# A hybrid trunk on one core: layer 3's block copies all on ScalarE, its chains' zero fills all on GpSimd

## The chip, the core and the metric

One core of a Trainium2 chip. The metric is the device time of one execution, in microseconds; the median of three runs stands for the kernel.

## The reference, cut to what matters

A trunk of four layers over 256 latent and 256 context tokens, width 1024, float32. Each layer has a token mixer (latent attention, differential attention, gated linear attention, gated DeltaNet) and a squared-ReLU MLP. The change lies in the mixer of layer 3, the gated delta rule, in chunks of 64 tokens, 16 value heads, both directions:

```
lmat  = where(strict, (k*beta) @ k^T * gamma, 0)         # 64x64 per chunk, head and direction
t_inv = triangular_solve(lmat, eye, lower, unit_diagonal) # its inverse
u, w  = t_inv @ (v*beta), t_inv @ (k*beta*exp(gc))
step:   v_new = u_c - w_c @ s;  o = q_c @ s + a_c @ v_new;  s = s*d_c + k_c^T @ v_new
```

The inverses are needed for 256 matrices of 64x64 (4 chunks, 16 heads, 2 directions, 2 streams of tokens), and the recurrence over chunks then uses them.

## The kernel before, in words

`run` goes through layers 0 to 2, then opens layer 3 with `gdn_products` and `gdn_scans`, and ends with the MLP of layer 3.

`gdn_products` makes the projections of layer 3 and solves for the inverses in two groups of eight heads. The projections come as jobs (k, q, v and z of one head each). A v job is 24 matmuls on TensorE (L296 to L298, weights split into a high and a low part by ScalarE's cast L279 and VectorE's subtraction L280), a convolution (L1387 on ScalarE, then four L1390 on VectorE), SiLU on ScalarE, four transposes on TensorE (L1585) and scalings on ScalarE (L1588), and a store by GpSimd's queue (L1589). A z job is eight matmuls (L1544) and a SiLU. `GDN_PLAN` says how many jobs the code puts beside each step of a solve.

`gdn_solve(grp)` has three parts.

- Setup. For each pass p (0 and 1: which half runs forward) and each pair of chunks t it masks the gates of eight heads on VectorE (L1408), sums them on TensorE (L1411), takes the exponential on ScalarE (L1413) and multiplies into the matrix `lm[p]` on VectorE (L1414, L1415). `lm[0]` lies in buffer `xd`, `lm[1]` in `xb`. Each 64x64 matrix is then taken apart into two 32x32 diagonal blocks (`xc`, in buffer `xa`, L1434) and one off-diagonal block (`lo`, L1436). One copy moves 32 partitions x 1024 elements. In L1434 ScalarE and VectorE copy in turn (q even: ScalarE, q odd: VectorE), four copies per pass; in L1436 one each per pass. Two transposes of VectorE (L1439) follow; they write `x`, which takes the buffer `xb` again and so has to wait until `lm[1]` has been read.
- Loop. 31 steps of forward substitution on VectorE (L1444 and L1446), with jobs beside them.
- Join. Four transposes on VectorE (L1450, L1451), then for both passes k small 32x32 matmuls on TensorE (L1460), evacuated by ScalarE (L1463), the diagonal blocks copied into the result `uc` (L1469: four copies per k, b = 0 on ScalarE, b = 1 on VectorE), zeros into its upper block by GpSimd (L1470), a second set of small matmuls (L1476), evacuated by ScalarE with a sign (L1478), and a store of `uc` to memory by GpSimd's queue (L1481).

`gdn_scans` opens its buffers, fills the zero halves of the block-diagonal tiles once (L1837: four `uc` tiles on VectorE, three `at` tiles on GpSimd, two fills of 64 partitions x 512 elements each), and runs the chains (`gdn_chain`), which load the stored `uc` into the other halves (L1618, SyncE's queue) and multiply with them on TensorE (L1653), with ScalarE (L1657) and VectorE (L1650, L1672) between.

The order of the instructions of an engine is not the order of the code. A planner orders each engine's queue when the program is built, by the place in the code, by when the operands are ready in its own model of costs, and by free buffers: in the trace the first copies of pass 0 (L1434) run from 2070.2 us on, before pass 1's products, which stand ahead of them in the code. Buffers are counted: three rows for the setup's products (`side`), two PSUM banks for the sums and the small matmuls (`st`).

Of the kernel before, what the change touches and what calls it, by code (L numbers as in the profile page):

```python
# [157 lines left out]
class Trunk:  # L158
# [1234 lines left out]
    def gdn_solve(self, grp):  # L1393


        nc = self.nc
        lm = [self.x4.tile([128, 32, 64], F32, name=("xd", "xb")[p]) for p in range(2)]
# [25 lines left out]
        xc, v = both("xa"), both("xc")  # L1423
        quad = lambda a, b: slice(64 * a + 32 * b, 64 * a + 32 * b + 32)

        lo = self.lpool.tile([128, 32, 32], F32, name="lo")
# [3 lines left out]
        for p in passes:  # L1430
            nc.gpsimd.memset(v[:, p].rearrange("p i j -> p (i j)")[:, ::33], 1.0)
            for q in range(4):
                b = 32 * (q % 2)
                (nc.vector.tensor_copy if q % 2 else nc.scalar.copy)(xc[32 * q:32 * q + 32, p], lm[p][32 * q:32 * q + 32, :, b:b + 32])  # L1434
            for a in range(2):
                (nc.vector.tensor_copy if a else nc.scalar.copy)(lo[quad(a, p)], lm[p][quad(a, p), :, 32 * (1 - p):32 * (1 - p) + 32])  # L1436
        x = both("xb")
        for p in passes:
            nc.vector.transpose(out=low(x[:, p], p), in_=sw(xc[:, p]))  # L1439
# [8 lines left out]
        un, ut = both("xd"), both("xa")  # L1448
# [16 lines left out]
        for k in passes:  # L1465
            uc = self.x4.tile([128, 32, 64], F32, name=("xc", "xa")[k])
            for a in range(2):
                for b in range(2):
                    (nc.vector.tensor_copy if b else nc.scalar.copy)(uc[quad(a, b), :, 32 * b:32 * b + 32], un[quad(a, b), k])  # L1469
                nc.gpsimd.memset(uc[quad(a, 1 - k), :, 32 * k:32 * k + 32], 0.0)  # L1470
            for u0 in (0, 16):
                zp = self.st.tile([128, T2], F32, name="st")
                for u in range(16):
                    for a in range(2):
                        src, dst = quad(a, 1 - k), quad(a, k)
                        nc.tensor.matmul(zp[dst, 32 * u:32 * u + 32], lhsT=y[src, k, u0 + u], rhs=un[src, k, u0 + u], start=True, stop=True)  # L1476
                for a in range(2):
                    nc.scalar.mul(uc[quad(a, k), u0:u0 + 16, 32 * (1 - k):32 * (1 - k) + 32],  # L1478
                                  zp[quad(a, k)].rearrange("p (u c) -> p u c", c=32), -1.0)
                yield  # L1480
            nc.gpsimd.dma_start(self.spill[f"uc{grp}{k}"], uc)  # L1481
# [340 lines left out]
    def gdn_scans(self):  # L1822
        nc = self.nc
        with ExitStack() as ctx:
            pool = self.opener(ctx)
            self.open_psum(pool, **GDN_BANKS)
            banks = self.accs
            self.acc = lambda: banks.tile([128, T2], F32, name="acc")
            self.vp, self.ktk = pool("gdnv", GDN_ROWS2[4]), pool("gdnkt", GDN_ROWS2[5])

            diag = pool("gdnd2", 1)
            self.diag = {}
            for name, n in (("uc", GDN_ROWS2[1]), ("at", GDN_ROWS2[2])):
                ts = [diag.tile([128, 2, 4, 2, 64], F32, name=f"{name}{j}") for j in range(n)]
                for x in ts:
                    for a in range(2):
                        (nc.vector if name == "uc" else nc.gpsimd).memset(x[64 * (1 - a):64 * (1 - a) + 64, :, :, a], 0.0)  # L1837
                self.diag[name] = cycle(ts)
            self.tmp = pool("gdng2", GDN_ROWS2[3])
            self.rows = lambda: self.tmp.tile([128, T2], F32, name="t512")  # L1840
            self.stp, self.sm = pool("gdns", GDN_ROWS2[0]), pool("gdnsm", 2)
            self.op = pool("gdno", 4)

            def together(*gens):

                due = [0.0] * len(gens)
                left = set(range(len(gens)))
                while left:
                    for j in sorted(left):
                        due[j] += gens[j][1]  # L1850
                        while due[j] >= 1 and j in left:
                            due[j] -= 1
                            if next(gens[j][0], left) is left:
                                left.remove(j)

            def gates():
                for h in self.zheads:
                    self.gdn_gate(h)
                    yield

            kinds = dict(z=gates, c=self.gdn_chain, f=self.gdn_finish, n=self.gdn_query_norms)
            lane = lambda jobs: chain.from_iterable(kinds[j[0]](*map(int, j[1:])) for j in jobs.split())
            for n, lanes in enumerate(GDN_LANES):
                if n == 1:
                    self.tables()
                    self.uctx.close()
                    right = lambda *a: pool(*a, side="right")
                    self.zp, self.yp = right("gdnz", 1), right("gdny", 1)
                    self.open_ln(right, S)
                    nc.sync.dma_start(self.z[:, :, :S], self.spill["residual"])  # L1870
                together(*((lane(jobs), rate) for jobs, rate in zip(lanes, GDN_RATES[n])))
            self.ln_finish(*LAT)
# [67 lines left out]
```

## Time and profile before

| | us |
|---|---|
| median of 3 runs (2747.2 to 2750.26) | 2747.46 |
| the profiled execution | 2742.15 |
| its span | 2740.4 |
| TensorE matmul busy | 2638.8 (96%) |
| VectorE busy | 2009.0 (73%) |
| ScalarE busy | 1251.6 (46%) |
| GpSimd busy | 46.2 (2%) |
| first solve: first copy to last store issued | 2070.2 to 2174.6 |
| second solve: first copy to last store issued | 2196.2 to 2297.2 |

The span runs from the first to the last instruction. Busy times overlap, since the engines work side by side. PE is TensorE, PEld its weight loads, DVE is VectorE, ACT ScalarE, POOL GpSimd, SP SyncE. The granted clock (PEclk) is a share of full speed, the mean over the stretch.

### The profile page before, as it was taken

The numbers are of one execution on the slowest core, as the hardware profiler recorded it, in microseconds if no ns is written. First come the engines' busy times: TensorE is split into PE (matmuls) and PEld (weight loads), VectorE is DVE, ScalarE is ACT, GpSimd is POOL, SyncE is SP. The second block draws the span as 40 slices with busy tenths as digits, with TensorE's granted clock in tenths as the row PEclk, the third lists the DMA queues.
The fourth block names the chain that finished last, engine by engine and source line by source line (L and its number), as shares of the span: only waits on it lengthen the run. The fifth ranks groups of instructions, "written<-read, shape, count | busy, mean of one in ns | idle before, by whom it ended". The sixth has DMA issues, their size and how long they took to land. (4 is left out here: it accounts for less than half of the span.)

```text
span 2740.4 us, 40940 instructions
## 1 busy us (share of the span) xinstructions
PE 2638.8 (96%) x15728; PEld 2135.9 (78%) x15728; DVE 2009.0 (73%) x3796; ACT 1251.6 (46%) x2413; POOL 46.2 (2%) x71
## 2 busy tenths in 40 slices
PE   7999999999999999999999999999999998997998
PEld 5666888878866687888888897888887776657997
DVE  3677898776667798785745589876689896669666
ACT  3555453224556653333445553332454545445544
POOL 0000000000000000000000000000000111000000
PEclk9999999999999999999999999999999998999999
DMA  6533156553221136554221126554323445314453
GB/s 236 171 118 127 51 175 197 189 176 117 65 65 52 41 116 222 183 187 127 67 70 62 62 76 225 191 178 151 100 85 106 155 154 155 91 28 136 157 183 111
DMA packets 125535, 353.25 MB, mean 129 GB/s; under 512 B 37499, under 2 KB 41339, under 8 KB 124828
## 3 DMA queue, kind: packets, MB, share of 16 engines
q1 hardware_dynamic: 121804, 337.00, 38.7%
q0 software_dynamic: 3536, 13.63, 1.4%
q8 instruction: 124, 2.03, 0.3%
q14 instruction: 71, 0.58, 0.1%
HBM read 335.91 MB, written 14.68 MB: 128 GB/s over the span
## 5 line engine op out<-in xcount | busy, mean ns | idle before, releaser
L279 ACT CAST whi<-raw 128x1024 fp32r<-128x1024 f32 (+2 forms) x403 | 410.5, 1023 | 698.0 <-PE acc L297 253.6
L280 DVE TENSOR_TENSOR wlo<-raw,whi 128x1024 fp32r<-128x1024 f32 (+2 forms) x403 | 478.0, 1189 | 208.0 <-ACT whi L279 196.1
L296 PE MATMUL pj<-ul,whi 128*128 128x512 f32 (+1 forms) x1072 | 394.8, 368 | 0.1
L297 PE MATMUL pj<-uh,whi 128*128 128x512 f32 (+1 forms) x1072 | 384.5, 359 | 0.0
L298 PE MATMUL pj<-uh,wlo 128*128 128x512 f32 (+1 forms) x1072 | 383.4, 358 | 0.7 <-DVE wlo L280 0.6
L450 DVE SCALAR_TENSOR_TENSOR acc<-raw,s,acc 128x1024 f32<-128x1024 f32 x252 | 317.3, 1280 | 33.3 <-DMA raw<-in_ada 29.9
L296 PE MATMUL acc<-ul,whi 128*128 128x512 f32 (+3 forms) x888 | 311.3, 351 | 17.7 <-DVE ul L566 10.6
L297 PE MATMUL acc<-uh,whi 128*128 128x512 f32 (+3 forms) x888 | 309.0, 348 | 0.0
L298 PE MATMUL acc<-uh,wlo 128*128 128x512 f32 (+3 forms) x888 | 307.6, 347 | 0.0
L296 PEld LDWEIGHTS pj<-ul,whi 128*128 128x128 f32 x1072 | 203.6, 190 | 36.3 <-issue 6.1
L298 PEld LDWEIGHTS pj<-uh,wlo 128*128 128x128 f32 x1072 | 203.0, 189 | 34.4 <-issue 5.4
L297 PEld LDWEIGHTS pj<-uh,whi 128*128 128x128 f32 x1072 | 203.4, 190 | 29.3 <-issue 5.2
L296 PEld LDWEIGHTS acc<-ul,whi 128*128 128x128 f32 (+2 forms) x888 | 167.4, 189 | 42.1 <-DVE ul L566 12.6
L296 PE MATMUL pj<-hl,whi 128*128 128x512 f32 (+1 forms) x560 | 198.3, 354 | 0.7 <-DVE hl L633 0.2
L297 PE MATMUL acc<-hh,whi 128*128 128x512 f32 (+1 forms) x560 | 197.5, 353 | 0.0
L298 PE MATMUL acc<-hh,wlo 128*128 128x512 f32 (+1 forms) x560 | 196.6, 351 | 0.5 <-DVE wlo L280 0.5
L297 PE MATMUL pj<-hh,whi 128*128 128x512 f32 (+1 forms) x560 | 196.8, 351 | 0.0
L296 PE MATMUL acc<-hl,whi 128*128 128x512 f32 (+1 forms) x560 | 196.8, 351 | 0.0
L298 PE MATMUL pj<-hh,wlo 128*128 128x512 f32 (+1 forms) x560 | 196.2, 350 | 0.0
L298 PEld LDWEIGHTS acc<-uh,wlo 128*128 128x128 f32 (+2 forms) x888 | 167.4, 189 | 21.8 <-issue 1.0
L297 PEld LDWEIGHTS acc<-uh,whi 128*128 128x128 f32 (+2 forms) x888 | 167.4, 189 | 20.8 <-issue 1.2
L632 ACT CAST hh<-t 128x512 fp32r<-128x512 f32 (+1 forms) x128 | 72.1, 567 | 123.7 <-DVE t L631 123.3
(463 smaller groups left out, 4890.2 us busy)
## 6 DMA issues: line engine op xcount, KB each, us to landing
raw<-in_w SPq DMA_DIRECT2D x256, 512.0 KB, 4.0
raw<-in_ada SPq DMA_DIRECT2D x192, 512.0 KB, 4.6
raw<-in_diff_qk SPq DMA_DIRECT2D x16, 512.0 KB, 3.4
raw<-in_gdn_v SPq DMA_DIRECT2D x16, 512.0 KB, 4.2
raw<-in_gdn_z SPq DMA_DIRECT2D x16, 512.0 KB, 4.4
raw<-in_gdn_out SPq DMA_DIRECT2D x16, 512.0 KB, 3.7
raw<-in_mla_in SPq DMA_DIRECT2D x9, 512.0 KB, 7.3
raw<-in_mla_qb SPq DMA_DIRECT2D x12, 384.0 KB, 3.9
```

The source lines that it names most:

```text
L279: nc.scalar.copy(hi[:, :width], raw[:, :width])
L280: nc.vector.tensor_sub(lo[:, :width], raw[:, :width], hi[:, :width].bitcast(F32))
L296: mm(ps, lhsT=ah, rhs=bl, start=start, stop=False)
L297: mm(ps, lhsT=ah, rhs=bh, start=False, stop=False)
L298: mm(ps, lhsT=al, rhs=bh, start=False, stop=stop)
L450: nc.vector.scalar_tensor_tensor(acc[r], w, self.s[:, k, r:r + 1], acc[r], op0=ALU.mult, op1=ALU.add)
L632: nc.scalar.copy(hh[:, f, :t], r[:, :t])
```

## The change

Three places. All copies of L1434, L1436 and L1469 are issued on ScalarE; before, half of them were on VectorE (20 of 40 over both solves). The zero fills of the four `uc` tiles (eight instructions, L1837) are issued on GpSimd with those of `at`.

```diff
@@ gdn_solve, setup
             for q in range(4):
                 b = 32 * (q % 2)
-                (nc.vector.tensor_copy if q % 2 else nc.scalar.copy)(xc[32 * q:32 * q + 32, p], lm[p][32 * q:32 * q + 32, :, b:b + 32])
+                nc.scalar.copy(xc[32 * q:32 * q + 32, p], lm[p][32 * q:32 * q + 32, :, b:b + 32])
             for a in range(2):
-                (nc.vector.tensor_copy if a else nc.scalar.copy)(lo[quad(a, p)], lm[p][quad(a, p), :, 32 * (1 - p):32 * (1 - p) + 32])
+                nc.scalar.copy(lo[quad(a, p)], lm[p][quad(a, p), :, 32 * (1 - p):32 * (1 - p) + 32])
@@ gdn_solve, join
                 for b in range(2):
-                    (nc.vector.tensor_copy if b else nc.scalar.copy)(uc[quad(a, b), :, 32 * b:32 * b + 32], un[quad(a, b), k])
+                    nc.scalar.copy(uc[quad(a, b), :, 32 * b:32 * b + 32], un[quad(a, b), k])
@@ gdn_scans
                     for a in range(2):
-                        (nc.vector if name == "uc" else nc.gpsimd).memset(x[64 * (1 - a):64 * (1 - a) + 64, :, :, a], 0.0)
+                        nc.gpsimd.memset(x[64 * (1 - a):64 * (1 - a) + 64, :, :, a], 0.0)
```

## Rows read from the trace of the kernel before

**Rows 1.** Busy time by stretch; columns: stretch, PE, PEld, DVE, ACT, POOL, PEclk, DMA.

```profile
2060.00:2150.00 90.00, 84.80 (x372) 68.30 (x371) 87.74 (x148) 43.90 (x89) 9.58 (x15) 0.98 0.41 129
2150.00:2180.00 30.00, 26.54 (x652) 21.35 (x651) 23.44 (x31) 18.34 (x28) 7.78 (x9) 0.89 0.40 145
2180.00:2274.00 94.00, 87.46 (x383) 68.74 (x382) 88.71 (x149) 46.23 (x99) 13.52 (x22) 0.98 0.47 151
2274.00:2300.00 26.00, 21.69 (x544) 19.44 (x544) 17.64 (x21) 17.40 (x32) 10.01 (x13) 0.54 0.63 186
```

**Rows 2.** Waits of PE, 2060 to 2315 us: total, times, longest.

```profile
PE acc L1544 <- DVE y L1390: 3.7, 1, 3.7
PE acc L296 <- DVE y L1390: 0.6, 1, 0.6
...
PE st L1460 <- DVE xa L1451: 2.0, 2, 1.5
PE st L1476 <- ACT xc L1478: 0.9, 1, 0.9
...
PE st L1411 <- DVE side L1408: 2.4, 1, 2.4
...
PE st L1460 <- DVE xa L1451: 1.9, 1, 1.9
```

**Rows 3.** Groups by line, 2060 to 2300 us: busy us, mean ns, idle before.

```profile
L1469 DVE COPY xc<-xd 32x1024 f32<-32x1024 f32 x4 | 4.2, 1051 | 0.1
L1469 DVE COPY xa<-xd 32x1024 f32<-32x1024 f32 x4 | 4.0, 995 | 2.5 <-PE st L1460 2.5
L1837 DVE MEMSET uc<- 64x512 f32 x8 | 3.9, 485 | 1.2 <-issue 0.5
L1434 DVE COPY xa<-xd 32x1024 f32<-32x1024 f32 x4 | 2.8, 688 | 0.1
...
L1469 ACT COPY xa<-xd 32x1024 f32<-32x1024 f32 x4 | 4.2, 1042 | 0.1
```

**Rows 4.** Busy time in four stretches of 10 us, columns as in rows 1.

```profile
2080.00:2090.00 10.00, 6.28 (x23) 4.91 (x22) 9.92 (x11) 9.74 (x16) 0.00 (x0) 0.85 0.46 143
2160.00:2170.00 10.00, 8.56 (x321) 7.15 (x313) 8.32 (x10) 9.61 (x14) 4.86 (x5) 0.95 0.29 85
2206.00:2216.00 10.00, 10.00 (x43) 8.15 (x44) 8.31 (x8) 9.92 (x22) 1.57 (x3) 0.83 0.62 192
2284.00:2294.00 10.00, 8.87 (x284) 8.15 (x278) 8.00 (x12) 8.83 (x17) 7.13 (x10) 0.50 0.42 117
```

**Rows 5.** Timeline of the first setup: start, us, engine, line, operation, idle before.

```profile
2074.26 4.05 PE L1544 MATMUL pj<-u,raw 128*128 128x256 f32 x18
...
2082.95 2.10 ACT L1434 COPY xa<-xb 32x1024 f32<-32x1024 f32 x2
...
2085.06 1.04 ACT L1436 COPY lo<-xb 32x1024 f32<-32x1024 f32 x1
...
2086.30 3.96 DVE L1439 STREAM_TRANSPOSE xb<-xa 128x1024 f32<-128x1024 f32 x2
...
2086.43 5.41 PE L1544 MATMUL acc<-u,raw 128*128 128x256 f32 x16 [3.72 <-DVE y L1390]
```

**Rows 6.** Chain that ended last, in the second setup: start, us, what.

```profile
2202.05 0.70 DVE lo L1436
...
2209.89 1.04 ACT xa L1434
2210.93 0.01 issue
2210.94 1.06 ACT lo L1436
```

**Rows 7.** Timeline of the second setup's end, as in rows 5.

```profile
2212.02 4.10 DVE L1439 STREAM_TRANSPOSE xb<-xa 128x1024 f32<-128x1024 f32 x2 [1.61 <-ACT lo L1436]
```

**Rows 8.** Timeline of the chains' start, as in rows 5.

```profile
2287.04 2.66 POOL L1837 MEMSET at<- 64x512 f32 x4
...
2294.01 2.08 PE L1653 MATMUL ax<-v,uc 128*128 128x128 f32 x8
...
2296.68 0.54 POOL L1481 DMA_DIRECT2D uc<-xa  x1 [3.11 <-issue]
```

## The prediction

> **What bounds the kernel now.** I read the profile from wide to narrow. First the busy time by stretch over the two solves of layer 3 [rows 1]. The reader is to see two kinds of stretch. In the substitution loops (2060 to 2150 and 2180 to 2274 us) TensorE is busy 94 and 93% and VectorE 97 and 94%, while ScalarE is busy 49% in both: two full engines and one half empty. In the joins (2150 to 2180 and 2274 to 2300) nobody is full, and TensorE, VectorE and ScalarE hand small pieces to each other. So a few microseconds of VectorE work are worth something in the loops and little in the joins.
>
> Second, what TensorE waits for there [rows 2]. Five waits name VectorE: 3.7 and 0.6 us for a convolution (L1390) at the end of the first solve's setup, 2.4 us for the gate product (L1408) in the second one, and 2.0 and 1.9 us for the transposes (L1451) that end the two loops. Together 10.6 us. After the first of them the clock is low: the 16 matmuls of L1544 took 5.41 us [rows 5], and the stretch shows a granted clock of 0.85 [rows 4].
>
> Third, ScalarE by ten microseconds just where the copies are [rows 4]. Its half-empty mean hides four full places: 9.74, 9.61, 9.92 and 8.83 us of 10. These are the ends of the two setups and the two joins, where all the copies of the change belong. Fourth, the chain of waits in the second setup [rows 6, 7]: it runs through ScalarE's copies into the VectorE transposes, which had already waited for ScalarE.
>
> **The change part by part.** The planner of the program orders every engine's queue anew, so I price places, not slots.
>
> *The setup copies (L1434, L1436).* Per solve, six VectorE copies of 0.69 us go (4.1 us) and six ScalarE copies of 1.04 us come (6.2 us) [rows 3]. Three belong to pass 0. They fall where ScalarE is half idle, and I cost them there at nothing; their cover is that idle half [rows 1], and without it the exponentials of L1413 would queue behind them for up to 3.1 us. Taking three copies off VectorE can bring pass 1's matrix forward by 3 x 0.69 = 2.1 us at most. The three of pass 1 lie on the path: ScalarE did three copies from 2082.95 to 2086.1 and VectorE the other three beside it, and the transposes followed at 2086.30 [rows 5]. With six in one row ScalarE needs 3.1 us more. Both transposes wait for all of them, because their result takes the buffer of pass 1's matrix. So the transposes start between 1.0 us (3.1 less 2.1, all of the lead handed on) and 3.1 us later (none of it). I take 1.5 in the first solve, where ScalarE also has a table load and SiLUs in front, and 1.0 in the second, where the last VectorE copy of pass 0 lies on the chain itself, at 2202.05 [rows 6]. Behind these copies in ScalarE's queue stand L1387 (the start of a convolution) and the weight casts of L279: VectorE's other work comes from just these, so it can hardly fill the wait.
>
> *The join copies (L1469).* Per solve four VectorE copies go and four ScalarE copies come, 4 x 1.04 = 4.2 us. The VectorE copies took 1.05 and 1.00 us instead of 0.69 [rows 3]. That side of the join is free of cost, since VectorE idles there [rows 1]. On ScalarE the copies stand between the PSUM evacuations of L1463 and L1478, for which TensorE's small matmuls wait (0.9 us in the first join already [rows 2]). Bounds: 0 us, if all fit into ScalarE's gaps (12 us of 30 in the first join, 9 of 26 in the second [rows 1]), and 4.2 us, if none does. Of the first join's densest ten microseconds ScalarE is busy 9.61, of the second's 8.83 [rows 4]: I take 1.5 and 1.0, nearer to the low end, because gaps lie behind the dense part.
>
> *The memsets (L1837).* Eight go from VectorE (3.9 us [rows 3]) to GpSimd. VectorE has nothing late there: 17.6 us busy of 26 [rows 1]. GpSimd did four of the same size in 2.66 us from 2287.04 [rows 8], so eight take 5.3 us and end near 2292.4, before the first matmul that reads them at 2294.01 [rows 8]. I cost them at 0. Behind them in GpSimd's queue stand the other memsets and the stores of L1481 and L1589, whose data the later chains read back much later. SyncE's queue is passed by nothing.
>
> *What VectorE gets back.* It loses 12.3 us of work before the second loop ends (two setups, one join). TensorE's waits of 3.7, 0.6 and 2.4 us should go, and with them the low clock. How much of that is kept? At most 10.6 us of waits; 1.8 us for the 16 matmuls (5.41 us, against 18 of the same in 4.05 us at the full clock, so 16 x (0.338 - 0.225) = 1.8); and about as much (1.7 us, 10 us at 0.83) in the second setup [rows 2, 4, 5]: 14.1 us. At least nothing: the matmuls of L1460 wait for the transposes that end the loop, the loop starts later than before, and what TensorE wins in front it waits for there. I take 2.0 us, nearer to nothing, because a loop that is VectorE's for 97% starts later.
>
> Sum: 1.5 + 1.0 + 1.5 + 1.0 - 2.0 = +3.0 us. The profiled execution took 2742.15 us (span 2740.4), so 2745.2; the median of the runs shown, 2747.46, stands 5.3 us above it, which gives 2750.5; I say 2750. A measurement of this kernel tells from no change what differs by more than 0.2%, 5.5 us. So the likeliest outcome is no difference.
>
> **Rivals.** *VectorE was the bound and its relief is kept.* For it: 97% in the loops, and every large wait of TensorE names VectorE [rows 1, 2]. Against it: ScalarE is full where the copies land [rows 4]. If TensorE runs ahead with projections and keeps all, -14.1 us, with the setups' least +2.0: 2735; with half of it kept and the joins hidden, 2742. The Trainium skill states it as a rule (Perfetto Trace Analysis, Optimizing Scalar/DVE Operations): where VectorE is saturated, handing work to ScalarE may pay although VectorE is the faster. By that rule the time would fall; the loops' 97% agrees with its condition, ScalarE's full places do not with its promise.
>
> *ScalarE becomes the bound at the four places.* The price is 3.1 us for each setup and 4.2 us for each join, +14.6: 2762. It decides from the point where ScalarE has no gap left between the copies and what TensorE or VectorE waits for; in the second setup VectorE already waited 1.6 us for ScalarE's last copy [rows 7]. Against it: gaps of some microseconds behind each join. The Trainium skill (ScalarE: Activation LUTs, Rules for kernel authors) advises VectorE rather than ScalarE for simple elementwise work; the rows agree in the price of one copy, and by that alone the time would rise.
>
> *The memsets come late.* The change may not do what it says for the chains' start: if the planner puts them behind the last store of L1481, issued at 2296.68 [rows 8], the first four end near 2299.9 and the matmul of 2294.01 waits some 5.9 us, on top of the sum above: 2756. The stores' wait for ScalarE speaks for it, their place in the code (after the memsets' data are free, before their use) against it.
>
> **How the numbers follow.** No difference 0.45 (between 2742 and 2753, likeliest 2750), the relief kept 0.24, ScalarE the bound 0.27, late memsets 0.04. Faster 0.24 and slower 0.31 are these sums. The range reaches to both bounds but leaves out their ends, the lowest 3 us and the highest 2: 2738 to 2760.
>
> **What would show it.** Right: ScalarE copies of 1.04 us, no VectorE copy at L1434, L1436, L1469; the transposes of L1439 waiting for ScalarE by several microseconds in both setups; TensorE's 3.7 and 2.4 us waits gone and a longer wait before L1460; L1478 ending later. Wrong: transposes that start earlier than 2086 and 2212 relative to the layer's start, TensorE's waits in these 250 us falling by over 8 us, or the matmuls of L1653 waiting for GpSimd.

## The result: slower, 1.0054, and the profile after

The changed kernel takes 2760.91 us (median of 4 runs, 2759.44 to 2764.34), the kernel before, run beside it, 2747.33 (4 runs): the ratio is 1.0054, 95% interval 1.0042 to 1.0067. It is slower by 13.6 us, just above the top of the range (2760) and almost exactly where the second rival put it (2762). The profiled execution took 2761.21 us, span 2759.4 us.

The page's busy times after:

```profile
PE 2644.0 (96%) x15728; PEld 2139.1 (78%) x15728; DVE 1988.3 (72%) x3768; ACT 1271.7 (46%) x2433; POOL 47.6 (2%) x79
```

ScalarE is still less than half busy in the whole span. The busy time by stretch over the two solves, as in [rows 1], where the first number behind the stretch is its length and the last one GB/s (everything stands some 3 us later here than before; that offset is there already before the first place where the orders differ, and is no part of the change):

```profile
2063.00:2153.00 90.00, 80.08 (x352) 65.23 (x351) 80.28 (x134) 46.50 (x89) 7.96 (x13) 0.94 0.35 114
2153.00:2186.00 33.00, 30.73 (x600) 24.86 (x598) 17.59 (x23) 24.08 (x34) 8.06 (x11) 0.84 0.43 143
2186.00:2286.00 100.00, 86.29 (x447) 68.53 (x444) 87.00 (x153) 51.30 (x106) 12.79 (x22) 0.93 0.45 144
2286.00:2316.00 30.00, 23.39 (x545) 19.58 (x545) 10.69 (x9) 23.60 (x40) 13.47 (x22) 0.58 0.68 199
```

VectorE has indeed become free (97 to 89% and 94 to 87% in the loops), and TensorE with it: 94 to 89%, 93 to 86%. What VectorE gave up was not filled. A part of this is the windows, which are 3 us longer in the join and 6 us longer in the second loop. The ten microseconds around the copies, as in [rows 4]:

```profile
2083.00:2093.00 10.00, 6.83 (x31) 5.51 (x29) 3.19 (x5) 9.45 (x13) 0.00 (x0) 0.98 0.58 195
2171.00:2181.00 10.00, 9.41 (x233) 7.50 (x234) 0.25 (x1) 9.71 (x13) 1.34 (x2) 0.66 0.44 157
2220.00:2230.00 10.00, 1.98 (x9) 1.99 (x10) 3.46 (x4) 9.90 (x16) 0.58 (x2) 0.50 0.31 105
2304.00:2314.00 10.00, 6.52 (x154) 5.74 (x148) 0.00 (x0) 9.80 (x14) 5.89 (x11) 0.50 0.73 212
```

ScalarE is full at all four places while VectorE does 3.19, 0.25, 3.46 and 0.00 us of work. In the second setup TensorE is busy 1.98 us of 10. Two timelines of ScalarE, VectorE and TensorE at the setups' ends show why. First solve (start, us, engine, line, operation, idle before), to be read beside [rows 5]:

```profile
2086.28 4.19 ACT L1434 COPY xa<-xb 32x1024 f32<-32x1024 f32 x4
2090.48 2.10 ACT L1436 COPY lo<-xb 32x1024 f32<-32x1024 f32 x2
...
2092.61 3.88 DVE L1439 STREAM_TRANSPOSE xb<-xa 128x1024 f32<-128x1024 f32 x2 [6.78 <-ACT lo L1436]
```

Second solve, beside [rows 6, 7]:

```profile
2219.61 1.28 ACT L233 ACT_TABLE_LOAD   x1
2220.91 0.42 ACT L233 ACTIVATE x<-y 128x256 f32<-128x256 f32 x1
2221.23 4.19 ACT L1434 COPY xa<-xb 32x1024 f32<-32x1024 f32 x4
2225.43 2.10 ACT L1436 COPY lo<-xb 32x1024 f32<-32x1024 f32 x2
2227.55 1.03 ACT L233 ACTIVATE x<-y 128x256 f32<-128x256 f32 x3
...
2228.02 1.97 PE L1585 MATMUL ax<-ident,x 128*128 128x128 f32 x8 [9.11 <-ACT x L233]
```

Six copies stand in one row of 6.3 us. The transposes of L1439 wait 6.78 us for the last of them (before they followed at once). In the second solve three SiLUs stand behind the row, and TensorE's transposes of L1585 wait 9.11 us for them. The waits, TensorE's first, then VectorE's (in total, times, longest):

```profile
PE ax L1585 <- ACT x L233: 11.4, 4, 9.1
PE acc L296 <- DVE y L1390: 8.8, 1, 8.8
PE ax L1623 <- ACT kt L1625: 4.0, 1, 4.0
PE st L1411 <- DVE side L1408: 3.3, 2, 2.6
```
```profile
DVE wlo L280 <- ACT whi L279: 22.7, 5, 19.8
DVE side L1506 <- ACT z L1557: 15.4, 1, 15.4
DVE xb L1439 <- ACT lo L1436: 13.3, 2, 6.8
```

Before, the five large waits of TensorE named VectorE [rows 2]; now the first and the third name ScalarE, and VectorE itself waits 51 us for ScalarE in three groups. The two longest of these (19.8 and 15.4 us) lie at the joins, where VectorE has little left to do; the 13.3 us stand in front of the loops.

**The solve as a chain.** Waits say who waited, not what it cost. So I also cut each profiled span at the same events: *setup* is from the first ScalarE copy of L1434 to the first transpose of L1439, *loop* from there to the first L1450, *join* from there to the end of the last L1478, *gap* from there to the first L1434 copy of the second solve, *rest* from the second join's end to the first subtraction of the last norm (L1880). Each number below is the difference of two such times of one profile (us), read to a tenth, so that it may be off by one or two tenths. The kernel with the memsets alone moved has the order of before on every engine except for those memsets, so its column beside that of before shows how far two executions of one order differ (3 us in the first join). These 3 us are TensorE's clock: before, then memsets alone, columns as in [rows 1], the same 541 matmuls in the first join at a granted clock of 0.90 and of 0.63 (full speed is 2.4 GHz; the clock moves between this level and 1.2 GHz):

```profile
2151.84:2173.49 21.65, 18.20 (x541) 14.43 (x542) 17.98 (x16) 16.85 (x24) 5.22 (x5) 0.90 0.36 125
2152.00:2176.76 24.76, 23.24 (x541) 18.87 (x542) 18.70 (x16) 16.70 (x24) 5.29 (x5) 0.63 0.31 109
```

The names of the other columns are those of the experiments.

| stage | before | memsets alone | setups alone | joins alone | ScalarE repeats | after | after, old order | before, new order |
|---|---|---|---|---|---|---|---|---|
| setup 1 | 16.1 | 16.1 | 19.1 | 15.9 | 19.0 | 19.2 | 19.7 | 17.2 |
| loop 1 | 65.6 | 65.1 | 66.0 | 65.1 | 65.8 | 66.1 | 65.8 | 66.3 |
| join 1 | 21.6 | 24.7 | 23.9 | 24.8 | 24.1 | 24.9 | 25.7 | 21.4 |
| gap | 22.7 | 22.6 | 24.2 | 26.8 | 24.1 | 25.9 | 23.1 | 26.9 |
| setup 2 | 15.9 | 15.8 | 17.6 | 15.1 | 19.7 | 18.1 | 19.6 | 15.5 |
| loop 2 | 58.6 | 58.4 | 57.0 | 57.7 | 57.5 | 57.6 | 58.2 | 57.7 |
| join 2 | 25.5 | 24.6 | 28.2 | 29.2 | 26.7 | 28.7 | 28.2 | 28.2 |
| rest | 433.1 | 433.2 | 436.0 | 436.6 | 437.9 | 434.2 | 440.0 | 434.2 |
| sum | 659.1 | 660.5 | 672.0 | 671.2 | 674.8 | 674.7 | 680.3 | 667.4 |

After against before: setups +3.1 and +2.2, joins +3.3 and +3.2 (the first of these no more than the two executions of one order differ by), gap +3.2, loops +0.5 and -1.0, rest +1.1: +15.6 us in all. The loops, where VectorE was 97 and 94% busy, are 0.5 us longer and 1.0 us shorter: hardly anything of VectorE's relief is kept there.

### The profile page after: what moved, and what is told of

The parts are those of the page before. It is cut to its first block, busy times and chain, and to the rows that moved or that the text cites. A ratio compares the mean times of both kernels' runs of the same rounds, so it can differ in the third digit from the quotient of the medians.

```text
span 2759.4 us, 40940 instructions
## 1 busy us (share of the span) xinstructions
PE 2644.0 (96%) x15728; PEld 2139.1 (78%) x15728; DVE 1988.3 (72%) x3768; ACT 1271.7 (46%) x2433; POOL 47.6 (2%) x79
## 5 line engine op out<-in xcount | busy, mean ns | idle before, releaser
L279 ACT CAST whi<-raw 128x1024 fp32r<-128x1024 f32 (+2 forms) x403 | 410.5, 1023 | 690.7 <-PE pj L297 251.9
L280 DVE TENSOR_TENSOR wlo<-raw,whi 128x1024 fp32r<-128x1024 f32 (+2 forms) x403 | 477.6, 1189 | 230.4 <-ACT whi L279 218.7
L296 PE MATMUL pj<-ul,whi 128*128 128x512 f32 (+1 forms) x1072 | 395.0, 369 | 0.1
L298 PE MATMUL pj<-uh,wlo 128*128 128x512 f32 (+1 forms) x1072 | 382.6, 357 | 0.4 <-DVE wlo L280 0.3
L296 PE MATMUL acc<-ul,whi 128*128 128x512 f32 (+3 forms) x888 | 312.7, 352 | 26.0 <-DVE ul L566 10.8
L298 PE MATMUL acc<-uh,wlo 128*128 128x512 f32 (+3 forms) x888 | 309.3, 348 | 0.1
L296 PEld LDWEIGHTS pj<-ul,whi 128*128 128x128 f32 x1072 | 203.2, 190 | 35.8 <-issue 6.6
L298 PEld LDWEIGHTS pj<-uh,wlo 128*128 128x128 f32 x1072 | 202.9, 189 | 33.4 <-issue 5.2
L296 PEld LDWEIGHTS acc<-ul,whi 128*128 128x128 f32 (+2 forms) x888 | 168.6, 190 | 50.6 <-DVE ul L566 12.8
L296 PE MATMUL pj<-hl,whi 128*128 128x512 f32 (+1 forms) x560 | 198.2, 354 | 1.5 <-DVE hl L633 1.1
L296 PE MATMUL acc<-hl,whi 128*128 128x512 f32 (+1 forms) x560 | 196.7, 351 | 0.0
L298 PE MATMUL acc<-hh,wlo 128*128 128x512 f32 (+1 forms) x560 | 196.6, 351 | 0.0
L298 PE MATMUL pj<-hh,wlo 128*128 128x512 f32 (+1 forms) x560 | 196.2, 350 | 0.0
L298 PEld LDWEIGHTS acc<-uh,wlo 128*128 128x128 f32 (+2 forms) x888 | 168.7, 190 | 21.9 <-issue 0.7
```

Source lines behind the costliest of these rows:

```text
L279: nc.scalar.copy(hi[:, :width], raw[:, :width])
L280: nc.vector.tensor_sub(lo[:, :width], raw[:, :width], hi[:, :width].bitcast(F32))
L296: mm(ps, lhsT=ah, rhs=bl, start=start, stop=False)
L298: mm(ps, lhsT=al, rhs=bh, start=False, stop=stop)
```

## The experiments

The theory after this reading: the solve is one chain, and the copies lie on it; ScalarE does them one after the other, in front of SiLUs and casts that feed the other two engines, and VectorE's freed time is idle time. Rivals: the late start of the loop alone counts; the convolution and projection order that the planner writes for the moved copies makes the loss. Where an expectation numbers its theories, the letters hold for that run alone. All medians are against runs of the kernel before on the same chip (2744 to 2746 us).

### Each part alone: setups, joins, memsets

Setups alone has the first hunk of the diff only, joins alone the second, memsets alone the third:

```
-  (nc.vector.tensor_copy if q % 2 else nc.scalar.copy)(xc[32 * q:32 * q + 32, p], lm[p][32 * q:32 * q + 32, :, b:b + 32])
+  nc.scalar.copy(xc[32 * q:32 * q + 32, p], lm[p][32 * q:32 * q + 32, :, b:b + 32])
-  (nc.vector.tensor_copy if a else nc.scalar.copy)(lo[quad(a, p)], lm[p][quad(a, p), :, 32 * (1 - p):32 * (1 - p) + 32])
+  nc.scalar.copy(lo[quad(a, p)], lm[p][quad(a, p), :, 32 * (1 - p):32 * (1 - p) + 32])
```

> Only the setup copies (L1434, L1436) go to ScalarE; the join copies and the zero fills stay as before. If ScalarE's queue is the cause, VectorE waits 6 to 7 us before the transposes of L1439 in both solves, and the time is 6 to 9 us above before (2753 to 2756). If the cause lies in the joins, at most 2 us above. If it is the planner's new order as a whole, the parts will not add up: this one, the joins alone and the fills alone will differ from the change's +13.6 us by more than 5 us in sum.

> Only the join copies (L1469) go to ScalarE. If ScalarE's queue is the cause, the evacuations of L1478 end 3 to 4 us later in each solve and the time is 5 to 8 us above before (2752 to 2755), with no new wait before L1439. If only the setups count, at most 2 us above before.

> Only the zero fills of the uc tiles (L1837) go to GpSimd. If ScalarE's queue is the cause of everything, within 1.5 us of before. If late fills hold the start of the chains, 4 to 6 us above before, with the matmuls of L1653 waiting for GpSimd.

Setups alone: 2756.18 us, 1.0042 (1.0026 to 1.0058). Joins alone: 2756.70, 1.0043 (1.0028 to 1.0057). Memsets alone: 2746.10, 1.0000 (0.9988 to 1.0013). So the memsets cost nothing, and the two other parts cost about 11 us each alone, both more than expected, 22 if they added, but 13.6 together. A likely reason, not shown, is that both are paid partly in the same places: the table has the second join at 28.2 with the setups alone, 29.2 with the joins alone, 28.7 with both. It also has 28.2 there with the new order alone, no copy moved, so the length of this join is not the moved copies' work only.

### Which pass of the setups

Only pass 0's copies (then only pass 1's) go to ScalarE:

```
+  (nc.vector.tensor_copy if p and q % 2 else nc.scalar.copy)(xc[32 * q:32 * q + 32, p], lm[p][32 * q:32 * q + 32, :, b:b + 32])
+  (nc.vector.tensor_copy if p and a else nc.scalar.copy)(lo[quad(a, p)], lm[p][quad(a, p), :, 32 * (1 - p):32 * (1 - p) + 32])
```

> Of the setup copies only the three of pass 0 go from VectorE to ScalarE in each solve; pass 1, the joins and the fills stay as before. If the loss of the setups comes from the row of six copies of pass 1, in front of the convolutions' first step (L1387) and the SiLUs in ScalarE's queue, this has no TensorE wait of 6 to 9 us and is between 3 us below and 2 us above before. If every copy moved to ScalarE costs about its share, half of the setups' loss: 4 to 6 us above.

> The counterpart: only the three copies of pass 1 go to ScalarE in each solve. If the row of six is the cause, VectorE waits 3 us or more before L1439 in both solves, TensorE waits 6 to 9 us in each setup, and the time is 8 to 12 us above before, as much as with both passes. If every moved copy costs its share, 4 to 6 us above.

Pass 0: 2745.56 us, 1.0006 (0.9997 to 1.0014). Pass 1: 2754.08, 1.0040 (1.0028 to 1.0052). All of the setups' loss comes from pass 1's copies, as the prediction had it: pass 0's three stand where ScalarE is half idle. With pass 0's copies moved, TensorE waits 5.7 us for L1390 in one piece where it had waited 3.7 and 0.6 [rows 2], and the time is the same: TensorE's wait in front of a loop is not by itself the loss. The rows on GpSimd, below, show the reverse of it.

### Is it ScalarE's row, or VectorE's relief?

The kernel before, in which ScalarE does VectorE's three pass 1 copies a second time (the same values to the same places):

```
 (nc.vector.tensor_copy if q % 2 else nc.scalar.copy)(xc[32 * q:32 * q + 32, p], lm[p][32 * q:32 * q + 32, :, b:b + 32])
+p and q % 2 and nc.scalar.copy(xc[32 * q:32 * q + 32, p], lm[p][32 * q:32 * q + 32, :, b:b + 32])
 (nc.vector.tensor_copy if a else nc.scalar.copy)(lo[quad(a, p)], lm[p][quad(a, p), :, 32 * (1 - p):32 * (1 - p) + 32])
+p and a and nc.scalar.copy(lo[quad(a, p)], lm[p][quad(a, p), :, 32 * (1 - p):32 * (1 - p) + 32])
```

> The kernel before, and on ScalarE the three copies of pass 1 that VectorE makes are made a second time (same values), so ScalarE has the row of six while VectorE is relieved of nothing. If the row in ScalarE's queue is the whole cause, the time is 8 to 13 us above before, as with pass 1's copies moved, and VectorE's relief was worth nothing. If VectorE's relief is worth something that hid a larger loss, 15 us above or more.

2756.27 us, 1.0050 (1.0036 to 1.0064). ScalarE has the long row and VectorE no relief, and the time is that of pass 1 alone (1.0040, the intervals overlap). The timeline of ScalarE and VectorE in the first solve:

```profile
2081.44 4.20 ACT L1434 COPY xa<-xb 32x1024 f32<-32x1024 f32 x4
2085.65 2.11 ACT L1436 COPY lo<-xb 32x1024 f32<-32x1024 f32 x2
```
```profile
2082.09 1.40 DVE L1434 COPY xa<-xb 32x1024 f32<-32x1024 f32 x2
2083.42 0.68 DVE L1436 COPY lo<-xb 32x1024 f32<-32x1024 f32 x1
...
2087.79 3.95 DVE L1439 STREAM_TRANSPOSE xb<-xa 128x1024 f32<-128x1024 f32 x2 [2.91 <-ACT lo L1436]
```

VectorE does its copies and then waits 2.91 us. Without them it would wait longer. The three copies that the change takes from VectorE in pass 1 are worth nothing.

### Does the start of the loop decide? Another buffer for the transposes

The transposes wait for all copies because their result takes pass 1's buffer. Two kernels give it another ("xd" for the transposed matrix and y, "xb" for the inverse), one with the change, one without:

```
-  x = both("xb")
+  x = both("xd")
```

> The changed kernel, with the transposed blocks x in the buffer of pass 0's matrix (xd) instead of pass 1's (xb), and un and y exchanged accordingly. If the transposes of L1439 wait for the whole row of ScalarE copies because their result takes pass 1's buffer, then the two copies of lo of pass 1 (2.1 us) no longer hold them and pass 0's transpose runs beside pass 1's copies: VectorE's waits before L1439 fall from 6.5 to 6.8 us to about 2 to 4.7 us, and the time falls by 3 to 7 us against the changed kernel (2754 to 2758). If the copies were not what the transposes wait for, no difference from 2761.

> The kernel before with the transposed blocks x in the buffer of pass 0's matrix. The transposes of L1439 can start 1 to 4 us earlier. If the start of the loop is what the time hangs on, 2 to 5 us below before. If TensorE's waits for the convolutions are, and not the loop's start, within 2 us of before.

With the change: 2754.85 us, 1.0041 (1.0024 to 1.0058). Without: 2750.15, 1.0019 (1.0009 to 1.0030), slower than with the late start. The loop starts 9.8 us after the first copy instead of 16.1 in the latter, but lasts 70.1 instead of 65.6 us, and the gap behind it 25.6 instead of 22.7. An early start is eaten by VectorE's other work, which then falls into the loop. This makes the theory "only the late start counts" unlikely, and it doesn't repair the change.

### Parts of the joins, and a mild version

Only the joins' second half (k = 1) on ScalarE, then pass 0, the first half (k = 0) and the memsets together (of the two only the first is shown), a version that I hoped would be free:

```
+  (nc.vector.tensor_copy if not k and b else nc.scalar.copy)(uc[quad(a, b), :, 32 * b:32 * b + 32], un[quad(a, b), k])
```

> Of the join copies only those of k = 1 go to ScalarE (two per solve). If the loss of the joins comes from the row of four copies of k = 1 that stands in ScalarE's queue between the evacuations of k = 0 and of k = 1 and ahead of the next stage's copies, most of the joins' loss is here: 6 to 12 us above before. If the joins' loss is a matter of total load, half: 4 to 6 us. If it is the planner's order, any value.

> The change without its two rows: pass 0's setup copies, the join copies of k = 0 and the zero fills move as in the change, pass 1's and those of k = 1 stay split. If the two rows are the cause, within 3 us of before. If total load on ScalarE is, 4 to 8 us above.

k = 1 alone: 2751.30, 1.0028 (1.0018 to 1.0037). The mild version: 2753.86, 1.0041 (1.0025 to 1.0057), a miss. Pass 0 and the memsets are free alone, so k = 0 seems to cost as much as k = 1; it was not run alone, and the parts above did not add. In both the second join is longer (27.8 and 27.2 us instead of 25.5), and the gap too (24.4 and 24.8 instead of 22.7).

### GpSimd in place of ScalarE

All the joins' copies, then pass 1's two L1436 copies, on GpSimd:

```
+  nc.gpsimd.tensor_copy(uc[quad(a, b), :, 32 * b:32 * b + 32], un[quad(a, b), k])
```

> All join copies (L1469) go to GpSimd, so ScalarE loses four of 1.04 us in each join and VectorE four. If ScalarE's queue is what the joins hang on, the mirror image of the joins' loss: 2 to 8 us below before, with L1478 ending earlier. If GpSimd's copies are slower than 3 us each they end after L1478, and delay only the stores. If the planner's order is the cause, no sign can be told.

> The kernel before with the two copies of lo of pass 1 on GpSimd, so that in each solve ScalarE's row is two copies instead of three and VectorE's two instead of three. If the row is what the setups hang on, the mirror image: the transposes start about 1 us earlier and the time is 1 to 4 us below before. If GpSimd's copies are delayed by VectorE's, no gain, or up to 3 us above.

Joins on GpSimd: 2747.59, 1.0007 (0.9996 to 1.0019), although GpSimd's copies are no faster than ScalarE's; the gain of 2 to 8 us that the mirror image promised did not come. The groups by line:

```profile
L1469 POOL COPY xc<-xd 32x1024 f32<-32x1024 f32 x8 | 10.1, 1260 | 18.4 <-DVE xa L1451 18.2
L1469 POOL COPY xa<-xd 32x1024 f32<-32x1024 f32 x8 | 8.2, 1031 | 0.4
```

Sixteen copies on an engine that has nothing else to do cost nothing; eight more copies on ScalarE, whose L1463 and L1478 TensorE waits for, cost 11 us. This points to ScalarE's queue and not to the copies' length, though the missing gain says that taking copies out of that queue gives nothing back. Pass 1's L1436 on GpSimd: 2744.73, 1.0002 (0.9993 to 1.0012); I had expected a gain of 1 to 4 us and found none.

### The row taken off ScalarE altogether

If the row in front of the SiLUs were the whole cause, pass 1's copies on GpSimd would bring the time back. Four kernels: before with pass 1's three ScalarE copies on GpSimd; that with the joins on ScalarE; the changed kernel, and the setups alone, with all six of pass 1 on GpSimd (the lines of the last two):

```
+  (nc.gpsimd.tensor_copy if p else nc.scalar.copy)(xc[32 * q:32 * q + 32, p], lm[p][32 * q:32 * q + 32, :, b:b + 32])
+  (nc.gpsimd.tensor_copy if p else nc.scalar.copy)(lo[quad(a, p)], lm[p][quad(a, p), :, 32 * (1 - p):32 * (1 - p) + 32])
```

> Pass 1's three ScalarE copies of each setup (3.1 us) go to GpSimd, VectorE's three stay. Theory A, it is the row of copies on ScalarE, in front of the SiLUs, that costs time: with the row of before already nearly covered, between -3 and +1 us against the kernel before. Theory B, what counts is when the first transposes of the setup can start: GpSimd's copies take as long as ScalarE's, so within 1 us of before.

> All the joins' copies go to ScalarE (which alone cost 11 to 12 us), and pass 1's three ScalarE copies of each setup to GpSimd. Theory A, the joins' loss arises in the second setup, because the SiLUs that should precede pass 1's row on ScalarE stand behind it: with the row gone from ScalarE at most +5 us. Theory B, it arises where the joins themselves wait for their copies: +9 to +13 us as before.

> The changed kernel with pass 1's six copies of each setup on GpSimd instead of ScalarE, a row as long (6.2 against 6.3 us). Theory A, ScalarE's queue held by the row makes the loss: about +3 to +6 us against before, at most half of the changed kernel's. Theory B, the late first transposes make it: +11 to +16 us, as the changed kernel.

> Setup copies of pass 0 all on ScalarE, of pass 1 all six on GpSimd; joins and memsets as before. Theory A, the queue of ScalarE: -1 to +4 us against before. Theory B, the late first transposes, which start as late as with six ScalarE copies: +9 to +12 us, as with all the setup copies on ScalarE.

All four are slower: 2750.76 (1.0024, 1.0015 to 1.0033), 2761.87 (1.0062, 1.0047 to 1.0077), 2771.72 (1.0097, 1.0084 to 1.0110) and 2764.90 (1.0074, 1.0060 to 1.0089). The theory that the held queue of ScalarE is all falls in its simple form. But theory B's range is exceeded in all four, too. The first two do not test what they should: their expectation took GpSimd's copies for as long as ScalarE's, and beside VectorE's copies they were longer, 1.39 to 1.55 us for five of the six (the first solve's first took 1.03), so that the setups grew to 17.9 and 16.7 us in the first of them. The second solve there:

```profile
2212.29 3.00 POOL L1434 COPY xa<-xb 32x1024 f32<-32x1024 f32 x2 [3.58 <-DVE xb L1415]
2215.35 1.39 POOL L1436 COPY lo<-xb 32x1024 f32<-32x1024 f32 x1
```

The last two have no VectorE copies in pass 1, and their GpSimd copies took 1.03 to 1.05 us. In the last of them the SiLUs and the convolution do go ahead of the copies, and TensorE's wait in the first setup is gone; ScalarE, then GpSimd, then TensorE and VectorE there:

```profile
2083.31 1.95 ACT L233 ACTIVATE kT<-y 128x256 f32<-128x256 f32 x6
```
```profile
2083.86 4.26 POOL L1434 COPY xa<-xb 32x1024 f32<-32x1024 f32 x4 [4.98 <-DVE xb L1415]
2088.18 2.14 POOL L1436 COPY lo<-xb 32x1024 f32<-32x1024 f32 x2
```
```profile
2088.62 0.47 PE L296 MATMUL acc<-ul,whi 128*128 128x512 f32 x1 [0.83 <-DVE y L1390]
...
2090.35 4.20 DVE L1439 STREAM_TRANSPOSE xb<-xa 128x1024 f32<-128x1024 f32 x2 [1.10 <-POOL lo L1436]
```

But the first setup is as long as with the ScalarE row (19.0 us), because six copies in one row take as long on GpSimd, and the loops are far longer: 73.6 and 67.1 instead of 65.6 and 58.6. Why the loops grow I can only describe: in the first one (2090 to 2165 us) VectorE does ten of the subtractions of L280, where before has eight (2086 to 2152), and it waits 4.5 us for ScalarE's casts of L279. The planner had written another order, and this left the last question.

### The copies or the order

All instructions keep their numbers when only an engine is exchanged, so one kernel's order can be laid on the other: behind the code that emits the program, each instruction of every queue, from the first place where the orders differ, is tied behind the one that it follows in the other kernel. The moved copies and fills and the loads of the function tables alone are left free (four matmuls of L1544 just ahead of the tied part changed their place among each other).

```
+  made = {i.name: i for i in nc.cur_bb.bb.instructions}
+  for queue in ORDER:
+      q = queue.split()
+      for a, b in zip(q, q[1:]):
+          tc.add_manual_dep(made["I-" + b], "I-" + a, mybir.DependencyInfo(
+              mybir.DependencyClass.NoSync, mybir.DependencyReason.DATA), reason="order")
```

> The changed kernel's copies and fills on their new engines, but every other instruction of every queue, from the first place where the orders differ, tied to the order that the kernel before has. Theory A, the copies themselves, waited for in ScalarE's queue, cost the time: +10 to +16 us against before. Theory C, it is the order that the scheduler writes when the copies have moved (independent matrix products spent in the joins and gone when TensorE waits behind the SiLU table load): 0 to +5 us. Between these, both have a share.

> The kernel before, copies and fills on their old engines, but every other instruction of every queue tied to the order of the changed kernel. Theory A: -2 to +4 us against before. Theory C: +9 to +15 us, although no copy has changed its engine.

| | old order | new order |
|---|---|---|
| copies and fills where they were | 1 | 1.0024 (1.0012 to 1.0036) |
| copies and fills moved | 1.0064 (1.0048 to 1.0079) | 1.0054 (1.0042 to 1.0067) |

The moved copies and fills in the old order cost as much as the change itself (2762.14 us against 2744.35), and the fills alone cost nothing. So the copies on ScalarE are enough to make the loss, without the new order. The new order alone costs 8.4 us (2752.74), more than theory A allowed (-2 to +4) and less than theory C asked for (+9 to +15); with the copies moved it adds nothing. The two losses do not add, and how they share the 13.6 us is open. No run ties a kernel to its own order, so what the ties themselves cost is not shown. In the old order the table shows the loss where the copies are: setups +3.6 and +3.7, joins +4.1 and +2.7, 14.1 us in all, gap +0.4, loops +0.2 and -0.4; another +6.9 in the rest is 433.1 against 440.0. These 6.9 us are TensorE's clock again, 7.0 us more of busy time for the same matmuls at 0.95 instead of 0.97 (before, then old order):

```profile
2296.14:2729.27 433.13, 404.03 (x2994) 343.05 (x2992) 296.44 (x744) 196.96 (x473) 1.62 (x3) 0.97 0.39 119
2310.12:2750.12 440.00, 411.02 (x2990) 348.84 (x2990) 296.49 (x743) 196.85 (x473) 1.63 (x3) 0.95 0.37 117
```

The first join's +4.1 is in large part the clock as well: it is 0.59 there, and against memsets alone (0.63) the difference is +1.0. All five executions of the old order with the moved copies have a mean granted clock of 0.977 to 0.979, the 15 of the kernel before beside them 0.979 to 0.987; whether the copies' waits lower it, no run shows. In the new order part of it stands in the gap instead (+3.2 in the changed kernel, +4.2 with the new order alone). The timeline of VectorE in the old order with the moved copies has the same waits in front of the loops as the changed kernel:

```profile
2089.51 3.88 DVE L1439 STREAM_TRANSPOSE xb<-xa 128x1024 f32<-128x1024 f32 x2 [5.47 <-ACT lo L1436]
...
2223.73 3.90 DVE L1439 STREAM_TRANSPOSE xb<-xa 128x1024 f32<-128x1024 f32 x2 [6.81 <-ACT lo L1436]
```

TensorE's waits show what the new order does. In the old order TensorE waits for SiLUs at L1585 only 2.9 us in the second setup, because 24 independent products (L296 to L298) stand between the last gate products of L1411 and the second group of these transposes, as in the kernel before. In the changed kernel none is left there; they had been placed earlier. TensorE's waits from 2212 to 2270 us with the moved copies in the old order:

```profile
PE st L1411 <- DVE side L1408: 3.3, 1, 3.3
PE ax L1585 <- ACT x L233: 2.9, 1, 2.9
```

The 9.1 us wait of the changed kernel is therefore the place where the loss is seen, not where it arises: with the products in their old place the wait is a third of it and the time no shorter. No version tried beats the kernel before.

## Why the prediction was wrong, step by step

**The setups.** The mechanism was right: transposes that wait for ScalarE by several microseconds (6.8 and 6.5 us), three copies more in one row. The size was not. "I take 1.5 in the first solve ... and 1.0 in the second" failed: measured +3.1 and +2.2, and +3.6 and +3.7 in the old order. The upper bound, three copies of 1.04 us, was the value to take, and the old order lies some 0.5 us above it. The reason given for the lower ones, that up to 2.1 us of lead from pass 0 would be handed on, is refuted in the first solve by its setup with pass 0 alone moved: 16.4 us, no shorter than 16.1. In the second solve a part was handed on: 14.4 us with pass 0 alone moved instead of 15.9, and 17.6 with both passes moved where pass 1 alone gives 20.2.

**The joins.** "I take 1.5 and 1.0, nearer to the low end, because gaps lie behind the dense part" failed for the second join: +2.7 in the old order, at the same clock (0.58) as before. The changed kernel's +3.2 agrees, but can't be put down to the copies alone, since the new order without them has 28.2 us, too. In the first one +3.3 and +4.1 stand against 3 us that the clock alone makes, so its size stays open between about 1 us and the upper bound of 4.2. Gaps behind a dense part are of no use to a chain that runs through the dense part.

**What VectorE gets back.** "TensorE's waits of 3.7, 0.6 and 2.4 us should go ... I take 2.0 us" failed in its sign. The waits went from these lines to others and grew (8.8, 9.1 and 4.0 us), with the low clock behind the first two, and repeating the three copies on ScalarE while VectorE keeps its own costs as much as moving them. VectorE's freed time became waiting time, 6.8 us of it right before the first loop. What should have told me stood in [rows 5, 7]: VectorE's transposes already followed the copies at once, or waited for ScalarE. An engine that is 97% busy in a loop gains nothing from work taken away ahead of the loop, if the loop can't start before another engine is done.

**The memsets** cost nothing, as predicted: alone 1.0000, and no matmul of L1653 waits for GpSimd. They came later than the 2292.4 us worked out for them: in the changed kernel the last of the eight ends at 2306.5, after the first matmuls of L1653 at 2304.4, which did not have to wait for it.

**Sum.** The forecast was +3.0 us. The prediction's terms with the values measured in the old order: setups 3.6 + 3.7, joins 4.1 + 2.7, memsets 0, VectorE's relief 0: +14.1 us, or 11.0 with +1.0 for the first join. The medians give 13.6 for the change and 17.8 for the moved copies in the old order; most of that remainder lies in the rest, at the lower clock, a term that the sum did not have. The second rival, 14.6, had the right path: its condition ("no gap left between the copies and what TensorE or VectorE waits for") holds at three of four places and at the first join perhaps. That its number is within 1 us of the measured one is in part luck, because the changed kernel pays 3.2 us of its loss in the gap and hardly more than 2 us in the second setup. The evidence for it was in [rows 4], ScalarE 9.74, 9.61, 9.92 and 8.83 us busy of 10, and I set its chance below that of no difference by taking each bounded term near its low end, four times in the same direction. The first rival, VectorE as the bound, would have shown shorter loops; they are 0.5 us longer and 1.0 us shorter. Its rule from the Trainium skill (Perfetto Trace Analysis, Optimizing Scalar/DVE Operations), that handing work from a saturated VectorE to ScalarE may pay, brought nothing here: VectorE was busy for 97% of the first loop, and the time rose by 0.54%.

## What to carry to other kernels

Where two engines share a set of copies that one consumer waits for, moving all to one engine can cost the whole added length of that engine's row, however free the engine is on average: look at its busy share in the ten microseconds before the consumer, and take the upper bound if that is full. Relief for a busy engine counts only from a point where that engine, and not the one that takes the work over, is waited for. When a planner writes the order, a large new wait may stand far from its cause: compare the lengths of the stages of the dependent chain, and lay the old order on the new kernel, before a wait is booked as the price. Compare the granted clock of each stage as well: a stage can grow by 3 us with no change in its work.

## What the runs showed of the hardware beyond that

GpSimd copies 32x1024 float32 in 1.03 to 1.05 us, as long as ScalarE (1.04), also while VectorE does the multiply-adds of L1390. Beside VectorE's copies it took 1.39 to 1.55 us, and beside VectorE's subtraction L280 1.94: two such copies make the mean of 1.26 in the group above. VectorE's copies, 0.69 us alone, mostly take longer beside GpSimd's memsets (up to 1.51 in the kernel before), and these longer beside them: with VectorE's copies gone, the memsets of L1470 take 1.92 us for two, where before the mean of one was 1.17:

```profile
2292.86 1.93 POOL L1470 MEMSET xc<- 32x1024 f32 x2 [5.54 <-DVE xa L1451]
2297.92 1.92 POOL L1470 MEMSET xa<- 32x1024 f32 x2 [3.13 <-PE st L1460]
```

After its wait of 8.8 us TensorE went on at the lower clock level: the matmuls of L296 to L298 followed each other at 0.43 instead of 0.23 us for 4 us (granted clock 0.52 from 2098.66 to 2103, the 1.2 GHz level of 1.2 and 2.4), while after a wait of 0.83 us in the kernel with the row on GpSimd they kept 0.23. And one order does not mean one time: medians of the kernel before in the six comparisons lie between 2744.35 and 2747.33 us, and single runs between 2735 and 2755. The time goes with the mean granted clock: 2735.31 us at 0.988 and 2754.95 at 0.979, and a line through the 107 runs of that kernel beside the experiments falls by 1.6 us per 0.001. By that estimate some 9 of the 17.8 us of the moved copies in the old order (0.978 against 0.983) and some 5 of the change's 13.6 (0.9805 against the 0.984 of those 107) go along with a lower clock; which is cause and which is effect, no run shows.
